# Six token chunks instead of three multiplied from the raw input in float32, at the start of a diffusion step

## The chip, the cores and the metric

The kernel runs on one core of a Trainium2 chip. The number that counts is the device time of one execution in microseconds; the kernel before takes 2201.28 us, the median of three runs from 2199.71 to 2201.73. A tenth of one per cent is therefore 2.2 us.

The engines are named as in the profile: PE (TensorE: matrix products; PEld its weight loads), DVE (VectorE), ACT (ScalarE), POOL (GpSimd) and SP, which issues nearly all of the transfers.

## The reference

One layer of a backbone works on 128 context tokens and 1024 latent tokens, 1152 in all, with 1024 channels. The layer starts like this, and this start is all that the change touches:

```python
sh1, sc1, gt1, sh2, sc2, gt2 = adaln(cond, p['w_mod'], p['b_mod'])   # silu(c) @ w_mod + b_mod
h = rmsnorm(x, p['g_norm_mix']) * (1.0 + sc1) + sh1
z = h @ p['w_in']        # columns: zq, zkv, zkpe, zmq, zmk, zmv, zgate, zmo, zbr
...
mv = zmv.reshape(B, S, MLSTM_HEADS, MLSTM_DV)     # 4 heads of 256 values
```

The context tokens have one modulation vector, the latent tokens another. After this come latent attention, a two-way chunked mLSTM that uses the values `mv`, a merge, a gated feed-forward block and a last norm.

Everything is float32, and the outputs are compared in float32. One value product for a chunk of 128 tokens and two heads is 128 x 1024 times 1024 x 512.

## The kernel before

**Two ways to multiply.** A product in float32 proper is one matmul instruction per 128 rows of the contraction. The other way splits each operand into a high part `h`, rounded to a shorter float32 (`hi`, line 69, on ACT), and the rest `l` (`lo`, line 75, on DVE), and adds three matmuls `h*h + h*l + l*h` (`mm3`, lines 98 to 100). The profile tells the two apart by their lines: L470 is the float32 product of the start, L98, L99 and L100 are the three of `mm3`.

**The nine chunks of the values.** `start` (line 329) makes the values of all nine 128-token chunks for two halves of the columns, `hp` 0 and 1: eighteen jobs, each of eight contraction steps `k`. They come in four groups, named in line 381 and put in order in line 382; each group runs over four pieces of weights, of 128 x 1024 and two steps `k` each:

- `GR`, half 0, chunks 1, 2, 3, from the raw input. For a latent token, `h` is `r * (x * A) + sh` with one factor `r` per token. So the product can be taken on raw `x` with the weights scaled by `A` (`ws`, line 510, ACT) before `r` is known, and `r` and the shift come in when the result leaves PSUM (`vout`, line 495, DVE). This group uses float32 proper (`rawmm`, L470).
- `GA`, half 1, chunks 5, 6, 7, split.
- `GB`, half 1, chunks 0, 1, 2, 3, 8, 4, split.
- `GC`, half 0, chunks 0, 5, 6, 7, 8, 4, split.

Chunk 4 lies across the middle of the tokens and is copied together by POOL (`copy4`, line 447, tile `c4`).

**What runs while.** The input arrives in four blocks `b` of two steps `k`, together with the modulation weights. For each block PE computes the modulation (`gemv`, lines 367 and 372), and ACT and DVE square the input for the norm (lines 403 and 405). After the last block, `stats` finds `r` (lines 411 to 420), and `modk` turns `x` into `h` in place: a multiplication on DVE (L435), an addition on ACT (L437), then `hi` and `lo`. The half of the tokens from 576 on (`j` = 1) is done first, since `GA` needs it; the other half is done while `GA` and `GB` run.

Results leave PSUM over three buffers `vs` (line 494) and SP's queue. PSUM has six banks for these products (`mm` in line 77). The weights of a piece have four split buffers, `wh` and `wl` of two pieces (`loadv`, line 392).

During `GB`, POOL also begins the four large differences of `t_ops` (line 568), which the next stage, `z_lat`, needs. The pieces of the next stage (`pair`, matmuls 128x288) follow directly on PE after `GC`.

**What sets the order.** The program is written in one stream; a scheduler with its own estimate of times then puts each engine's instructions into a fixed order. An engine works through its list strictly in that order, except for what the hardware overlaps. So a change of three lines can move instructions well away from those lines.

Of the kernel before, what the change touches and what calls it, by code (L numbers as in the profile page):

```python
# [19 lines left out]
P = 128  # L20
D = 1024
KD = 8
# [25 lines left out]
GT = T // 2  # L48
# [8 lines left out]
class K:  # L57
# [271 lines left out]
    def start(self, vp):  # L329


        nc, a, pp = self.nc, self.a, self.pp
# [14 lines left out]
        xv = lambda k, j: X[k // 4][j][:, k % 4]  # L347
# [30 lines left out]
                                        self.vec[:, self.V_GMIX + k:self.V_GMIX + k + 1], op0=ALU.add, op1=ALU.mult)  # L378
            nc.vector.tensor_copy(shs[:, 2 * b:2 * b + 2, 0:1], self.mod1[:, 2 * b:2 * b + 2, 1:2])
        nc.scalar.activation(sil[:, :, 0:2], self.silc, AF.Silu)  # L380
        GR, GA, GB, GC = (1, 2, 3), (5, 6, 7), (0, 1, 2, 3, 8, 4), (0, 5, 6, 7, 8, 4)
        order = [(0, GR, kk) for kk in range(4)] + [(hp, g, kk) for hp, g in ((1, GA), (1, GB), (0, GC)) for kk in range(4)]
        raw, wv = {}, {}

        def vload(i):
            if i < len(order):
                hp, _, kk = order[i]
                raw[i] = self.wp.tile([P, 4 * DV], F32, name=self.nm("wr"), tag="wr", bufs=self.wb[0])
                nc.sync.dma_start(raw[i], a["w_v"][hp][:, kk * 4 * DV:(kk + 1) * 4 * DV])

        def loadv(i):
            if i < len(order):
                w = [self.wp.tile([P, 4 * DV], R32, name=self.nm(n), tag="wo", bufs=self.wb[1]) for n in ("wh", "wl")]
                r = raw.pop(i)
                self.last = self.hi(w[0], r), self.lo(w[1], r, w[0])
                wv[i] = [t.rearrange("p (k f) -> p k f", k=2) for t in w]
# [34 lines left out]
        def modk(k, j):  # L431
            x = xv(k, j)
            for c, s in ((slice(0, TP), 0), (slice(TP, GT), 1)) if j == 0 else ((slice(0, GT), 1),):
                A, sh = self.A1[:, k, s:s + 1], self.mod1[:, k, s:s + 1]
                line("s", lambda: nc.vector.scalar_tensor_tensor(x[:, c], x[:, c], A, rbc[:, j * GT + c.start:j * GT + c.stop],  # L435
                                                                 op0=ALU.mult, op1=ALU.mult).ins, "l")
                line("a", lambda: nc.scalar.activation(x[:, c], x[:, c], AF.Identity, bias=sh).ins, "h")  # L437
            nm = f"B{k // 4 + 1}{j + 1}"
            if nm not in self.hop:
                self.hop[nm] = tuple(self.slot({"B11": 0, "B21": 8, "B22": 10}[nm] + e, [P, 4, GT], nm) for e in range(2))  # L440
            h, l = self.hop[nm]
            line("h", lambda: self.hi(h[:, k % 4], x))
            line("l", lambda: self.lo(l[:, k % 4], x, h[:, k % 4]))

        def copy4(k, j):
            for e in range(2):
                nc.gpsimd.tensor_copy(c4[:, e, k, 64 * j:64 * j + 64],
                                      self.hop[f"B{k // 4 + 1}{j + 1}"][e][:, k % 4, 0 if j else GT - 64:64 if j else GT])
# [7 lines left out]
        ps = {}  # L456

        def vmm(w, c, k):
            if k == 0:
                ps[c] = self.bank(pp, "mm")  # L460
            self.mm3(ps[c], hc(k, c), (w[0][:, k % 2], w[1][:, k % 2]), k == 0, k == KD - 1)

        def rawmm(b, sw, e):

            w = sw.rearrange("p (k f) -> p k f", k=2)
            k = 2 * b + e
            for c in GR:
                if k == 0:
                    ps[c] = self.bank(pp, "mm")
                nc.tensor.matmul(ps[c], xv(k, 0)[:, c * P:(c + 1) * P], w[:, e], start=k == 0, stop=k == KD - 1)  # L470

        shv = sp.tile([P, 512], F32, name="shv")

# [18 lines left out]
        def vout(hp, c, r=None, sh=None):  # L492
            vs = vp.tile([P, 2 * DV], F32, name=self.nm("vs"), tag="vs", bufs=3)
            if r is not None:
                nc.vector.scalar_tensor_tensor(vs, ps[c], r[:, c:c + 1], sh, op0=ALU.mult, op1=ALU.add)
            elif c % 2:
                nc.vector.tensor_copy(vs, ps[c])
            else:
                nc.scalar.copy(vs, ps[c])
            nc.sync.dma_start(self.d_v[c, :, 2 * hp:2 * hp + 2, :], vs.rearrange("p (h v) -> p h v", h=2))  # L500
# [4 lines left out]
        for b in range(4):  # L505
            gemv(b)
            sw = f32v(self.wp.tile([P, 4 * DV], R32, name=self.nm("ws"), tag="wo", bufs=self.wb[1]))
            for e in range(2):
                k = 2 * b + e
                nc.scalar.activation(sw[:, 512 * e:512 * e + 512], raw[b][:, 512 * e:512 * e + 512], AF.Copy, scale=self.A1[:, k, 1:2])  # L510
            square(b)
            rawmm(b, sw, 0)
            if b == 3:
                st = stats()
                r = next(st)
            rawmm(b, sw, 1)
            shift(b)
            raw.pop(b)
            vload(b + 4)
# [11 lines left out]
        for i in range(4, 12):  # L531
            if i > 4:
                vload(i + 3)
            loadv(i + 1)
            for k in (2 * (i % 4), 2 * (i % 4) + 1):
                if i < 8:
                    modk(k, 0)
                    copy4(k, 0)
                    copy4(k, 1)
                for c in order[i][1]:  # L540
                    vmm(wv[i], c, k)
            if i % 4 == 3:
                for c in order[i][1]:
                    vout(1, c)
        es.close()
        xp = es.enter_context(self.pool("x"))
        self.push(self.t_ops(X, xp))
        for i in range(12, len(order)):
            hp, g, kk = order[i]
# [1546 lines left out]
```

## Time and profile before

| | us |
|---|---|
| median of three runs | 2201.28 |
| the profiled execution | 2201.13 |
| its span, first to last instruction | 2199.4 |
| up to the first raw product | 16.7 |
| raw products of four blocks (`GR`) | 41.5 |
| bridge to the first split product | 7.9 |
| `GA` (72 split matmuls) | 18.7 |
| `GB` (144) | 38.0 |
| `GC` (144) | 32.6 |
| all that follows | 2044.0 |

In the rows of the profile, the first number is the start in us from the start of the span, the second the duration; `xN` is how many instructions a row merges, and the bracket at the end tells how long the engine had been idle before, and what ended that. A float32 matmul shows up as two records. The share of PE's clock that was granted is `PEclk`, 1.00 at full speed.

### The profile page before, as it was taken

The numbers are of one execution on the slowest core, as the hardware profiler recorded it, in microseconds if no ns is written. First come the engines' busy times: TensorE is split into PE (matmuls) and PEld (weight loads), VectorE is DVE, ScalarE is ACT, GpSimd is POOL, SyncE is SP. The second block draws the span as 40 slices with busy tenths as digits, with TensorE's granted clock in tenths as the row PEclk, the third lists the DMA queues.
The fourth block names the chain that finished last, engine by engine and source line by source line (L and its number), as shares of the span: only waits on it lengthen the run. The fifth ranks groups of instructions, "written<-read, shape, count | busy, mean of one in ns | idle before, by whom it ended". The sixth has DMA issues, their size and how long they took to land.

```text
span 2199.4 us, 36807 instructions
## 1 busy us (share of the span) xinstructions
PE 2057.0 (94%) x13495; PEld 1873.4 (85%) x13495; DVE 1528.7 (70%) x2700; ACT 935.4 (43%) x1850; POOL 996.6 (45%) x766
## 2 busy tenths in 40 slices
PE   7899989999989888999999999889999999989897
PEld 3689989989978775667776899879999999989897
DVE  3846656988744977566664648899645555799895
ACT  3533334555455534333433335544322222456464
POOL 0622124667435414444446535576776733421501
PEclk9999999999989997999999999899999999999898
DMA  8332335555489685222224664223556512557664
GB/s 314 103 120 83 104 99 162 164 175 187 143 284 326 198 271 153 70 78 71 84 72 116 209 206 145 76 95 123 189 171 196 176 61 85 173 168 253 220 203 129
DMA packets 233795, 343.89 MB, mean 156 GB/s; under 512 B 20079, under 2 KB 166735, under 8 KB 232463
## 3 DMA queue, kind: packets, MB, share of 16 engines
q1 hardware_dynamic: 225070, 331.88, 47.3%
q0 software_dynamic: 4848, 6.06, 1.1%
q10 hardware_dynamic: 3696, 3.61, 0.5%
q8 instruction: 106, 1.74, 0.3%
q14 instruction: 75, 0.61, 0.1%
HBM read 253.69 MB, written 87.80 MB: 155 GB/s over the span
## 4 chain that ended last, share of the span: by engine, by line
PE 47%; DVE 11%; DMA 8%; POOL 6%; issue 5%; ACT 1%; SPq 1%; DVEq 0%; POOLq 0%; ACTq 0%
PE mm L98 11%; PE mm L100 11%; PE mm L99 11%; DVE wo L75 4%; PE pv L1476 3%; DMA pr<-w_fo 3%; PE st L98 2%; PE st L99 1%; PE st L100 1%; PE mx L1398 1%; DVE sm L1400 1%; PE p L1102 1%; PE p L1107 1%; PE p L1104 1%; POOL ps L1773 1%
## 5 line engine op out<-in xcount | busy, mean ns | idle before, releaser
L100 PE MATMUL mm<-th,wo 128*128 128x288 f32 x1840 | 547.3, 298 | 15.1 <-DVE wo L75 14.8
L98 PE MATMUL mm<-th,wo 128*128 128x288 f32 x1840 | 548.7, 298 | 3.0 <-DVE zo L1702 1.1
L99 PE MATMUL mm<-tl,wo 128*128 128x288 f32 x1840 | 547.0, 297 | 0.0
L100 PEld LDWEIGHTS mm<-th,wo 128*128 128x128 f32 x1840 | 349.6, 190 | 19.2 <-DVE wo L75 18.6
L75 DVE TENSOR_TENSOR wo<-wr,wo 128x512 fp32r<-128x512 f32 (+1 forms) x317 | 315.0, 1009 | 54.5 <-ACT wo L69 51.7
L98 PEld LDWEIGHTS mm<-th,wo 128*128 128x128 f32 x1840 | 348.6, 189 | 4.9 <-issue 1.6
L99 PEld LDWEIGHTS mm<-tl,wo 128*128 128x128 f32 x1840 | 349.2, 190 | 0.1
L69 ACT ACTIVATE wo<-wr 128x512 fp32r<-128x512 f32 (+1 forms) x317 | 187.5, 608 | 141.6 <-PE mm L100 62.5
L75 DVE TENSOR_TENSOR wo<-ws,wo 128x512 fp32r<-128x512 f32 x188 | 187.9, 1002 | 64.8 <-ACT wo L69 64.7
L69 ACT ACTIVATE wo<-ws 128x512 fp32r<-128x512 f32 x188 | 116.5, 626 | 270.8 <-PE mm L100 158.1
L1445 POOL TENSOR_TENSOR es<-es,p 128x512 f32<-128x512 f32 x112 | 157.1, 1402 | 91.0 <-ACT p L1438 87.2
L100 PE MATMUL mm<-xh,wo 128*128 128x288 f32 x616 | 184.5, 301 | 9.0 <-DVE wo L75 8.9
L99 PE MATMUL mm<-xl,wo 128*128 128x288 f32 x616 | 184.6, 300 | 0.0
L98 PE MATMUL mm<-xh,wo 128*128 128x288 f32 x616 | 183.9, 299 | 0.2 <-ACT wo L69 0.2
L1686 POOL TENSOR_TENSOR ws<-wr,ws 128x512 f32<-128x512 f32 x47 | 61.8, 1316 | 226.6 <-DVE wo L75 221.2
L1438 ACT ACTIVATE p<-st 128x512 f32<-128x512 f32 (+1 forms) x152 | 87.6, 578 | 158.0 <-PE st L100 146.4
L1400 DVE TENSOR_REDUCE sm<-mx 128x1 f32<-128x384 f32 (+1 forms) x200 | 99.1, 539 | 66.0 <-PE mx L1398 65.1
L98 PE MATMUL mm<-B,wo 128*128 128x288 f32 x456 | 134.8, 296 | 2.2 <-DVE zo L1702 1.3
L100 PE MATMUL mm<-B,wo 128*128 128x288 f32 x456 | 134.8, 296 | 0.0
L99 PE MATMUL mm<-B,wo 128*128 128x288 f32 x456 | 134.8, 296 | 0.0
L722 POOL TENSOR_TENSOR wm<-wm,sr 128x512 f32<-128x512 f32 x64 | 100.8, 1578 | 65.4 <-DVE mj L721 63.4
L100 PEld LDWEIGHTS mm<-xh,wo 128*128 128x128 f32 x616 | 118.0, 192 | 11.5 <-DVE wo L75 11.2
(436 smaller groups left out, 5067.5 us busy)
## 6 DMA issues: line engine op xcount, KB each, us to landing
wr<-w_ff SPq DMA_DIRECT2D x56, 512.0 KB
wm<-wm SPq DMA_DIRECT2D x32, 512.0 KB
wr<-d_w SPq DMA_DIRECT2D x32, 512.0 KB
d_z<-zo SPq DMA_DIRECT2D x48, 288.0 KB
d_g<-uu SPq DMA_DIRECT2D x44, 288.0 KB
wr<-w_big SPq DMA_DIRECT2D x24, 512.0 KB
wr<-w_fo SPq DMA_DIRECT2D x24, 512.0 KB
pr<-w_fo SPq DMA_DIRECT2D x40, 256.0 KB
```

Source lines behind the costliest of these rows:

```text
L69: i = self.nc.scalar.activation(out, in_, AF.Copy)
L75: return self.nc.vector.tensor_sub(out, in_, f32v(hi)).ins
L98: mm(out, lhs[0], rhs[0], start=first, stop=False)
L99: mm(out, lhs[0], rhs[1], start=False, stop=False)
L100: self.pe = mm(out, lhs[1], rhs[0], start=False, stop=last).ins
L722: nc.gpsimd.tensor_tensor(w[:, n], w[:, n], sr[:, 1], op=ALU.mult)
L1102: self.pe = mm(p1, A[:, h], V[:, h], start=True, stop=not carried).ins
L1400: self.iv = nc.vector.tensor_reduce(sm[:, t, j:j + 1], s[:, :kc], axis=AX.X, op=ALU.max, negate=True).ins
L1438: self.ia = nc.scalar.activation(p[:, :n], st[:, :n], AF.Exp).ins
L1445: nc.gpsimd.tensor_tensor(U["sum"], U["sum"], p, op=ALU.add)
L1476: self.pe = nc.tensor.matmul(pv[g * AV:(g + 1) * AV, q0:q0 + w], v[:, kb[c]], U["P"][c][:, q0:q0 + w], start=c < 2, stop=c == U["nc"] - 1, ...
L1686: G.tensor_tensor(s4, a12, s2, op=ALU.subtract)
```

## The change

```diff
-        GR, GA, GB, GC = (1, 2, 3), (5, 6, 7), (0, 1, 2, 3, 8, 4), (0, 5, 6, 7, 8, 4)
-        order = [(0, GR, kk) for kk in range(4)] + [(hp, g, kk) for hp, g in ((1, GA), (1, GB), (0, GC)) for kk in range(4)]
+        GR, GA, GB, GC = (1, 2, 3, 5, 6, 7), (5, 6, 7), (0, 8, 4), (0, 1, 2, 3, 8, 4)
+        order = [(0, GR, kk) for kk in range(4)] + [(hp, g, kk) for hp, g in ((1, GA), (0, GB), (1, GC)) for kk in range(4)]
...
             for c in GR:
                 if k == 0:
                     ps[c] = self.bank(pp, "mm")
-                nc.tensor.matmul(ps[c], xv(k, 0)[:, c * P:(c + 1) * P], w[:, e], start=k == 0, stop=k == KD - 1)
+                j = int(c > 4)
+                nc.tensor.matmul(ps[c], xv(k, j)[:, c * P - j * GT:(c + 1) * P - j * GT], w[:, e], start=k == 0, stop=k == KD - 1)
...
             if i % 4 == 3:
                 for c in order[i][1]:
-                    vout(1, c)
+                    vout(order[i][0], c)
```

Chunks 5, 6, 7 of half 0 move from the split `GC` to the raw `GR`, which now fills all six banks. `GB` keeps three chunks of half 0; the six-chunk group is the last one, of half 1. Eighteen jobs stay eighteen; six are raw instead of three.

**PE, the second block of the start.** `mm_209` to `mm_219` are the accumulators of `GR`, `ws` its scaled weights, `mx` with `wm` the modulation product of the next block. Before:

```order
L470 MATMUL mm_209<-ws_245,x_17_141 128x512
L470 MATMUL mm_211<-ws_245,x_17_141 128x512
L470 MATMUL mm_213<-ws_245,x_17_141 128x512
L367 MATMUL mx_268<-wm_165,sil 32x512 x4
L372 MATMUL mx_279<-vec,rows_277 128x2 x4
```

and now:

```order
L471 MATMUL mm_209<-ws_254,x_17_141 128x512
L471 MATMUL mm_211<-ws_254,x_17_141 128x512
L471 MATMUL mm_213<-ws_254,x_17_141 128x512
L471 MATMUL mm_215<-ws_254,x_18_142 128x512
L471 MATMUL mm_217<-ws_254,x_18_142 128x512
L471 MATMUL mm_219<-ws_254,x_18_142 128x512
L372 MATMUL mx_294<-vec,rows_292 128x2 x4
```

Six raw matmuls per step `k` stand where three stood, and the second part of the modulation product, which stood between the raw products and L372, has moved ahead of the raw products.

**DVE, after the last raw product.** `vs` is a result on its way out, `x` times `A` and `rbc` the multiplication of `modk`, `b12l` the first low part that `GA` uses. Before:

```order
L495 SCALAR_TENSOR_TENSOR vs_435<-mm_213,y_358,shv 128x512
L418 TENSOR_SCALAR dg_408<-ident,y_358 128x128
L435 SCALAR_TENSOR_TENSOR x_18_142<-x_18_142,A_70,rbc 128x576 x2
L75 TENSOR_TENSOR b12l<-x_18_142,b12h 128x576
L435 SCALAR_TENSOR_TENSOR x_18_142<-x_18_142,A_70,rbc 128x576
```

and now:

```order
L496 SCALAR_TENSOR_TENSOR vs_462<-mm_213,y_382,shv 128x512
L418 TENSOR_SCALAR dg_435<-ident,y_382 128x128
L496 SCALAR_TENSOR_TENSOR vs_465<-mm_215,y_382,shv 128x512
L435 SCALAR_TENSOR_TENSOR x_18_142<-x_18_142,A_70,rbc 128x576 x2
L496 SCALAR_TENSOR_TENSOR vs_468<-mm_217,y_382,shv 128x512
L496 SCALAR_TENSOR_TENSOR vs_471<-mm_219,y_382,shv 128x512
L75 TENSOR_TENSOR b12l<-x_18_142,b12h 128x576
```

The fourth result goes out ahead of the first `modk`, the fifth and sixth ahead of the first low part.

**DVE, at the end of `GA`.** `vs_642` before and `vs_678` now are the first result of `GA`, the `wl` the low parts of weight pieces, `B` those of the modulated input, all for `GB`. Before:

```order
L497 COPY vs_642<-mm_477 128x512
L75 TENSOR_TENSOR B_82_470<-x_17_141,B_81_469 128x576
L435 SCALAR_TENSOR_TENSOR x_19_143<-x_19_143,A_70,rbc 128x128
L435 SCALAR_TENSOR_TENSOR x_19_143<-x_19_143,A_70,rbc 128x448
L497 COPY vs_648<-mm_485 128x512
L75 TENSOR_TENSOR wl_654<-wr_552,wh_653 128x1024
```

and now:

```order
L498 COPY vs_678<-mm_513 128x512
L75 TENSOR_TENSOR B_88_506<-x_17_141,B_87_505 128x576
L435 SCALAR_TENSOR_TENSOR x_17_141<-x_17_141,A_70,rbc 128x128
L435 SCALAR_TENSOR_TENSOR x_17_141<-x_17_141,A_70,rbc 128x448
L498 COPY vs_684<-mm_521 128x512
L75 TENSOR_TENSOR wl_690<-wr_588,wh_689 128x1024
L75 TENSOR_TENSOR B_88_506<-x_17_141,B_87_505 128x576
```

When `GA`'s first result goes out, DVE has one step `k` more of the modulated input still to make than before: the low part in the row behind it is that of `k` = 1, where it was that of `k` = 2.

Far behind, between 640 and 840 us of the profile, where the mLSTM and the attention's projections share PE, some 300 of the 12,800 matmuls stand in another order too, though no line of that stage is changed. But for one further pair of rows, nothing else on PE moves.

## The prediction

> **What bounds the kernel now.** I read the busy time by stage first, since the change sits in the first 160 us.
>
> ```profile
> 16.70:58.20 41.50, 38.27 (x153) 16.73 (x151) 17.39 (x51) 15.77 (x24) 0.00 (x0) 0.96 0.76 297
> 58.20:66.10 7.90, 3.55 (x21) 2.44 (x20) 5.03 (x7) 4.10 (x8) 0.00 (x0) 0.86 0.49 166
> 66.10:84.80 18.70, 18.65 (x73) 15.23 (x74) 18.02 (x27) 16.52 (x26) 12.60 (x20) 0.88 0.17 57
> 84.80:122.80 38.00, 34.36 (x146) 27.90 (x144) 25.64 (x23) 13.57 (x23) 29.38 (x17) 0.96 0.32 103
> 122.80:155.40 32.60, 32.60 (x145) 27.02 (x144) 14.74 (x11) 14.78 (x13) 3.83 (x3) 1.00 0.31 100
> ```
>
> After the length come the busy times of PE, PEld, DVE, ACT, POOL, then PE's clock. These stages are GR, the bridge, GA, GB, GC. In GR, PE is busy 38.3 of 41.5 us: only 3.2 us are free to take more raw products. GC is pure PE work. In GA, DVE is nearly as full as PE. Next, what PE waits for, in order of time:
>
> ```profile
> 16.73 6.79 PE L470 MATMUL mm<-ws,x 128*128 128x512 f32 x12
> 29.48 5.42 PE L470 MATMUL mm<-ws,x 128*128 128x512 f32 x12
> 41.56 1.26 ACT L403 ACTIVATE sqs<-x 128x576 f32<-128x576 f32 x2 [0.24 <-DMA x<-xT]
> 36.65 1.05 PE L372 MATMUL mx<-vec,rows 128*128 128x2 f32 x8 [0.76 <-ACT rows L369]
> 47.22 1.05 PE L372 MATMUL mx<-vec,rows 128*128 128x2 f32 x8 [0.76 <-ACT rows L369]
> 52.07 6.19 PE L470 MATMUL mm<-ws,x 128*128 128x512 f32 x12
> 66.15 0.79 PE L98 MATMUL mm<-wh,b12h 128*128 128x512 f32 x1 [3.32 <-ACT b12h L69]
> 105.14 0.79 PE L99 MATMUL mm<-wl,B 128*128 128x512 f32 x1 [3.64 <-DVE wl L75]
> ```
>
> The last input has landed by 41.6 us, yet the last raw products start at 52.1: the loads do not pace this phase, PE's own list does. The one wait inside GB, 3.64 us, is for a low part from DVE. Behind GC, PE goes straight on, and most of the remaining stages are dense on PE, so I pass a shift at 155.4 us to the end.
>
> **The raw products.** What one costs:
>
> ```profile
> 54.23 0.19 PEld L470 LDWEIGHTS mm<-ws,x 128*128 128x128 f32 x1 [0.24 <-issue]
> 56.38 0.19 PEld L470 LDWEIGHTS mm<-ws,x 128*128 128x128 f32 x1 [0.24 <-issue]
> 122.80 0.39 PE L98 MATMUL mm<-wh,B 128*128 128x512 f32 x1
> 155.44 0.29 PE L98 MATMUL mm<-B,wo 128*128 128x288 f32 x1
> ```
>
> Five records lie between the first two rows: 2.15 / 5 = 0.43 us each, and a float32 product has two (12 records for 6 products above): 0.853 us with 0.4267 a record. GC's 144 matmuls take 155.44 - 122.80 = 32.64 us: 0.2267 each, 0.68 for a split product. Three chunks of eight steps move, 24 products: **24 x 0.853 = 20.5 us** go into GR, 24 x 0.68 = **16.3 us** come off the split groups. So even in full exchange PE has 4.2 us more to do.
>
> What of the 20.5 is hidden? The two waits of 0.76 for ACT's `rows` copy go: the modulation product now stands ahead of the raw products, which cover the copy. Minus 1.5. The rest of the 3.2 us free (waits on A, the scaled weights) has the same order as before. **GR ends 19.0 us later**; bounds 17.3 (all free time filled) and 20.5.
>
> **The bridge.** Six results go out instead of three, over three buffers.
>
> ```profile
> 59.97 2.07 DVE L495 SCALAR_TENSOR_TENSOR vs<-mm,y,shv 128x512 f32<-128x512 f32 x3 [0.39 <-ACT shv L490]
> 63.17 1.55 DVE L435 SCALAR_TENSOR_TENSOR x<-x,A,rbc 128x576 f32<-128x576 f32 x2 [0.94 <-ACT rbc L420]
> 66.13 0.76 DVE L75 TENSOR_TENSOR b12l<-x,b12h 128x576 fp32r<-128x576 f32 x1 [1.41 <-ACT b12h L69]
> 152.24 0.59 ACT L499 COPY vs<-mm 128x512 f32<-128x512 f32 x1 [0.43 <-PE mm L100]
> 155.14 0.69 DVE L497 COPY vs<-mm 128x512 f32<-128x512 f32 x1 [1.53 <-DMA d_v<-vs]
> ```
>
> The last two rows price a buffer: filled at 152.83, free at 155.14, 2.3 us. Measured on the times of before, the first buffer is full at 60.7 and free at 63.0, the fourth result takes 0.7, and the first modulation starts at 63.75 instead of 63.17: **+0.6**, and the first split matmul with it. The fifth and sixth (1.4 us) fit the hole of 1.41 ahead of the first low part; without that cover they would cost up to 1.4 more.
>
> **GB.** Its 72 matmuls would take 16.3 us instead of 32.6, and 3.64 of wait could go as well. But what GB needs is made while it runs, and there POOL stands in DVE's way:
>
> ```profile
> 87.47 0.68 DVE L497 COPY vs<-mm 128x512 f32<-128x512 f32 x1
> 88.07 5.58 DVE L75 TENSOR_TENSOR wl<-wr,wh 128x1024 fp32r<-128x1024 f32 x1
> 94.28 0.94 DVE L435 SCALAR_TENSOR_TENSOR x<-x,A,rbc 128x128 f32<-128x128 f32 x2
> 95.14 0.75 DVE L75 TENSOR_TENSOR B<-x,B 128x576 fp32r<-128x576 f32 x1
> 95.81 0.94 DVE L435 SCALAR_TENSOR_TENSOR x<-x,A,rbc 128x128 f32<-128x128 f32 x2
> 96.67 5.71 DVE L75 TENSOR_TENSOR B<-x,B 128x576 fp32r<-128x576 f32 x1
> 105.72 1.25 DVE L75 TENSOR_TENSOR wl<-wr,wh 128x1024 fp32r<-128x1024 f32 x1
> 115.70 2.77 DVE L75 TENSOR_TENSOR wl<-wr,wh 128x1024 fp32r<-128x1024 f32 x1 [8.74 <-ACT wh L69]
> ```
>
> ```profile
> 87.02 5.55 POOL L568 TENSOR_TENSOR t<-x,x 128x2304 f32<-128x2304 f32 x1
> 96.21 5.55 POOL L568 TENSOR_TENSOR x<-x,x 128x2304 f32<-128x2304 f32 x1
> 107.03 5.13 POOL L568 TENSOR_TENSOR x<-x,t 128x2304 f32<-128x2304 f32 x1
> 112.24 5.16 POOL L568 TENSOR_TENSOR t<-x,x 128x2304 f32<-128x2304 f32 x1
> ```
>
> Three times a DVE subtraction that meets one of POOL's large differences ends 1.1 us or less after it: 93.65 behind 92.57, 102.38 behind 101.76, 118.47 behind 117.40. So each difference stops DVE for some 5.1 us. Before, GB had 38 us to swallow two of them.
>
> The Trainium skill (SBUF — State Buffer, "Who interferes with whom") states the rule: a DVE instruction with two SBUF inputs and a GpSimd one share a port pair, whoever starts first holds it to its end, and issue order decides. The three overlaps agree; if DVE always came first, the sum would go towards the first rival.
>
> Now DVE's new order, still on the times of before. GA ends at 84.8 + 0.6 = 85.35, and its first result goes out to 85.85. Steps, from start to start in the rows: a pair of modulations 0.86, a low part 0.7; a copy 0.6; a weight's low part 1.15 (1.25 in its row, less the 0.1 by which rows overlap). To 89.85: low part, pair, copy, weight, low part. By then the first half of `x` is complete (ACT adds after the pair), and POOL's first difference holds DVE to 95.05. Pair, weight, low part, pair: 98.6. The second difference: 103.75. Four low parts, two pairs, a weight: 109.4, the last operand of GB. POOL copies chunk 4's piece and starts the third difference at about 110. PE still has GB's last ten matmuls, and only then are the buffers of the weights two pieces back free for GC's first piece: ACT makes the high part by 112.4, DVE's low part waits for POOL until 115.2 and ends at 116.4. Ahead of that PE has done five high products, so 139 x 0.2267 = 31.5 remain, and 1.3 for PE's clock:
>
> ```profile
> 64.00:66.00 2.00, 0.00 (x0) 0.00 (x0) 0.72 (x1) 1.98 (x3) 0.00 (x0) 0.50 0.39 148
> 66.00:68.00 2.00, 1.85 (x4) 1.49 (x5) 1.87 (x3) 1.02 (x3) 1.84 (x3) 0.50 0.00 0
> 107.44 0.63 PE L98 MATMUL mm<-wh,B 128*128 128x512 f32 x1
> 107.86 0.59 PE L99 MATMUL mm<-wl,B 128*128 128x512 f32 x1
> ```
>
> After a pause the clock is at 0.50, matmuls come 0.42 apart, and after the pause at 101 this lasted from 105.14 to 108.3, some 6.5 matmuls at 0.2 too much. GC then ends at 116.4 + 31.5 + 1.3 = 149.2, where it ended at 155.4: **-6.2**, with the 0.6 in it. Bounds: without any wait 85.35 + 216 x 0.2267 = 134.3, that is -21.1; with the fourth difference also ahead of the weight, +5.2, that is -1.0.
>
> **The mLSTM stage**, whose order moved, I take at nothing: what is swapped are independent products of the same size.
>
> ```profile
> 600.00:640.00 40.00, 30.07 (x201) 29.63 (x200) 17.18 (x31) 15.40 (x38) 12.86 (x19) 0.83 0.75 245
> 640.00:840.00 200.00, 182.09 (x981) 155.25 (x981) 139.75 (x415) 103.86 (x304) 68.68 (x60) 0.95 0.85 268
> ```
>
> PE idles 17.9 us in 640 to 840. A reorder can take at most that; as a loss I bound it by a few of PE's waits there, 4 us.
>
> **Sum**: +19.0 - 6.2 = **+12.8 us**. The profiled execution took 2201.13 us (1.7 around its span), 0.15 below the median: 2201.3 + 12.8 = **2214 us**.
>
> **The rivals.**
> - *The exchange goes through.* POOL's differences fall where DVE has nothing that PE waits for, GB and GC run densely: 19.0 - 21.1 = -2.1, 2199 us, no change. For it: DVE copies from PSUM pass beside POOL (87.47 within 87.02 to 92.57), and the weights of GB's third piece come earlier in DVE's order than before. Against: three overlaps of three stopped a subtraction, and even without POOL, DVE's steps above take 13.8 us of the 16.3 that GB would last, so any meeting shows. One difference out of the way gives +7.7.
> - *The port goes to POOL twice in a row* before GC's first low part: +18.0, 2219 us. For it: the fourth difference followed the third by 0.08 us. Against: DVE waits already when the third ends.
> - *The other side: the reordered mLSTM stage gains.* If PE's 17.9 idle us there closed up, 2214 - 17.9 = 2196 us, faster; it decides from 17.2 us on. For it: 300 rows moved there. Against: its transfers run at 268 GB/s, and a new order brings no data earlier.
> - *A wait behind absorbs the delay.* PE idles 9.9 us in 600 to 640; if its end were set by something that does not hang on PE's front, 2214 - 9.9 = 2204, no change. Against: one list after the other is fed by PE's results.
>
> That raw work hides behind the loads I rule out (41.56 against 52.07); and the order of PE shows that the change does what it says.
>
> **How the numbers follow.** Forecast 0.63, POOL twice 0.17, the exchange 0.10, the absorbed delay 0.05, the mLSTM gain 0.05. About 0.2%, 4.4 us, is what a measurement here tells from no change. Slower: 0.80 with both slower cases. Same: 0.15. Faster: 0.05. The forecast's own range is +7 to +17, with one difference more or less and GR's bounds; for 8 in 10 I add the POOL case above and some of the exchange below: 2202 to 2221.
>
> **What would show it.** Right: 96 records of raw products (L471 in the new numbering), the last raw products ending near 77 us; the first split matmul near 86; two DVE subtractions of over 5 us inside GB and a wait of PE for a low part at GC's start; the first 128x288 matmul near 168. Wrong: GR shorter than 58 us (raw products cheaper or hidden), GB near 16 us (POOL not in the way), or a difference that arises behind 168 us.

## The result and the profile after

The changed kernel takes 2220.24 us, the median of four runs from 2214.56 to 2221.53, beside 2201.51 us for the kernel before: a ratio of 1.0080, 95% interval 1.0061 to 1.0099. A second set of six runs gave 2216.95 us beside 2202.23, a ratio of 1.0067 (1.0051 to 1.0083). So the change makes the kernel 15 to 19 us slower. The first profiled execution took 2219.8 us, with a span of 2218.0.

The windows of the changed kernel, cut at its own stages (raw group, bridge, `GA`, `GB`, `GC`; the columns are those of the prediction's first fence):

```profile
15.70:75.40 59.70, 57.99 (x201) 26.55 (x199) 17.21 (x51) 15.82 (x25) 0.00 (x0) 0.95 0.55 213
75.40:85.50 10.10, 3.54 (x21) 2.43 (x20) 7.01 (x10) 4.11 (x8) 0.00 (x0) 0.88 0.45 156
85.50:104.00 18.50, 18.46 (x72) 15.11 (x73) 16.77 (x24) 15.23 (x23) 11.78 (x19) 0.88 0.27 87
104.00:135.40 31.40, 23.40 (x80) 16.90 (x79) 27.65 (x25) 16.33 (x27) 23.36 (x18) 0.84 0.32 108
135.40:166.50 31.10, 31.10 (x138) 25.72 (x138) 18.28 (x10) 12.76 (x10) 10.48 (x4) 1.00 0.28 94
```

The raw group now fills 59.7 us, where it filled 41.5. The fourth stretch takes 31.4 us with PE busy for only 23.4: that is where half of the 16.3 us taken off the split groups is given back. (It ends where PE goes on at 135.4; `GC`'s first matmul stands at 131.76, so `GB` itself takes 27.7 us.) PE's rows in order of time:

```profile
15.72 11.82 PE L471 MATMUL mm<-ws,x 128*128 128x512 f32 x24
63.90 1.05 PE L479 MATMUL mx<-wr,shs 128*32 128x512 f32 x4
64.88 10.57 PE L471 MATMUL mm<-ws,x 128*128 128x512 f32 x24
85.54 0.79 PE L98 MATMUL mm<-wh,b12h 128*128 128x512 f32 x1 [5.52 <-ACT b12h L69]
113.82 0.79 PE L100 MATMUL mm<-wh,B 128*128 128x512 f32 x1 [3.06 <-DVE B L75]
122.93 0.50 PE L100 MATMUL mm<-wh,B 128*128 128x512 f32 x1 [2.88 <-DVE B L75]
134.89 0.49 PE L99 MATMUL mm<-wl,B 128*128 128x512 f32 x1 [1.68 <-DVE wl L75]
166.54 0.29 PE L98 MATMUL mm<-B,wo 128*128 128x288 f32 x1
```

Four blocks of 24 records are the 48 raw products; the last ends at 64.88 + 10.57 = 75.45. In the fourth stretch PE waits three times for over 1 us for a low part from DVE, twice in `GB` and once at the start of `GC`, and what holds DVE stands in DVE's and POOL's rows:

```profile
77.16 2.07 DVE L496 SCALAR_TENSOR_TENSOR vs<-mm,y,shv 128x512 f32<-128x512 f32 x3 [0.39 <-ACT shv L491]
81.90 0.75 DVE L496 SCALAR_TENSOR_TENSOR vs<-mm,y,shv 128x512 f32<-128x512 f32 x1 [2.48 <-DMA d_v<-vs]
108.09 5.67 DVE L75 TENSOR_TENSOR B<-x,B 128x576 fp32r<-128x576 f32 x1
117.25 5.63 DVE L75 TENSOR_TENSOR B<-x,B 128x576 fp32r<-128x576 f32 x1
131.74 9.19 DVE L75 TENSOR_TENSOR wl<-wr,wh 128x1024 fp32r<-128x1024 f32 x2 [3.42 <-ACT wh L69]
```

```profile
107.60 5.55 POOL L569 TENSOR_TENSOR t<-x,x 128x2304 f32<-128x2304 f32 x1 [0.64 <-DMA d_v<-vs]
116.79 5.47 POOL L569 TENSOR_TENSOR x<-x,x 128x2304 f32<-128x2304 f32 x1
128.58 5.17 POOL L569 TENSOR_TENSOR x<-x,t 128x2304 f32<-128x2304 f32 x1
133.83 6.02 POOL L569 TENSOR_TENSOR t<-x,x 128x2304 f32<-128x2304 f32 x1
```

The two subtractions of 5.67 and 5.63 us end at 113.76 and 122.88, each 0.6 us behind one of POOL's differences, and PE goes on 0.05 us later, as predicted.

The first 128x288 matmul starts 11.1 us later than before. The kernel ends 18.6 us later. So in this execution 7.5 us arise behind the part that was changed, and they are the main question of the experiments. To place them, the same instruction of PE was looked up in each trace and in the first trace of before; the table gives the difference of its start in us (the middle one of all the instructions in the stretch, which is on the times of before). It holds all the profiles, those of the experiments too; `changed, again` and `before, again` are second executions of the two kernels.

| kernel | at 70 (`GA`) | 156 to 170 | 1000 to 1150 | 1480 to 1540 | 1750 to 1850 | 2100 to 2190 |
|---|---|---|---|---|---|---|
| changed | 19.3 | 11.1 | 9.0 | 12.2 | 18.2 | 18.8 |
| changed, again | 24.7 | 16.8 | 12.2 | 11.8 | 17.0 | 14.7 |
| before, again | 0.4 | 0.5 | 0.6 | 0.6 | 0.6 | 0.6 |
| raw_extra | 17.9 | 19.8 | 18.9 | 19.1 | 23.2 | 24.5 |
| order_3_6_3 | 20.8 | 7.2 | 7.7 | 10.6 | 15.4 | 14.4 |
| late_diff | 19.5 | 6.8 | 2.9 | 5.4 | 11.7 | 11.9 |
| late_diff_before | -0.8 | -0.9 | -4.3 | -3.6 | -4.0 | -4.5 |
| before_prep_once | 1.0 | 0.6 | -1.5 | -1.3 | -3.7 | -5.7 |
| after_prep_once | 19.9 | 11.7 | 9.7 | 13.3 | 10.5 | 9.4 |
| after_pad12 | 19.1 | 10.9 | 5.5 | 5.7 | 7.2 | 5.3 |
| before_pad24 | 1.3 | 1.4 | 1.3 | 1.9 | 4.6 | 7.5 |
| before_pad40 | 0.0 | 0.1 | -3.4 | -1.7 | 3.3 | 6.6 |
| before_pad52 | -0.1 | -0.1 | -3.6 | -3.0 | 3.2 | 4.2 |

### The profile page after: what moved, and what is told of

It is laid out like the page before. It is cut to its first block, busy times and chain, and to the rows that moved or that the text cites. A ratio compares the mean times of both kernels' runs of the same rounds, so it can differ in the third digit from the quotient of the medians.

```text
span 2218.0 us, 36751 instructions
## 1 busy us (share of the span) xinstructions
PE 2064.8 (93%) x13471; PEld 1870.4 (84%) x13471; DVE 1534.1 (69%) x2701; ACT 935.7 (42%) x1849; POOL 998.1 (45%) x766
## 3 DMA queue, kind: packets, MB, share of 16 engines
q8 instruction: 106, 1.74, 0.3%
## 4 chain that ended last, share of the span: by engine, by line
PE 48%; DVE 12%; DMA 8%; POOL 6%; issue 5%; ACT 2%; SPq 1%; DVEq 0%; POOLq 0%; ACTq 0%
PE mm L98 11%; PE mm L100 11%; PE mm L99 11%; DVE wo L75 5%; PE pv L1477 3%; DMA pr<-w_fo 3%; PE st L98 2%; PE st L99 2%; PE st L100 2%; PE mx L1399 1%; PE p L1103 1%; POOL wm L723 1%; DVE sm L1401 1%; DMA wm<-wm 1%; PE p L1105 1%
## 5 line engine op out<-in xcount | busy, mean ns | idle before, releaser
L100 PE MATMUL mm<-th,wo 128*128 128x288 f32 x1840 | 547.7, 298 | 14.2 <-DVE wo L75 13.9
L69 ACT ACTIVATE wo<-ws 128x512 fp32r<-128x512 f32 x188 | 116.4, 626 | 278.6 <-PE mm L100 146.9
```

The costliest lines, as they stand in the source:

```text
L69: i = self.nc.scalar.activation(out, in_, AF.Copy)
L100: self.pe = mm(out, lhs[1], rhs[0], start=False, stop=last).ins
```

## The experiments

### The raw products alone, and the order of the groups

The first kernel leaves before as it is and adds 24 raw products whose results nobody uses. The second is the changed kernel with the groups in the old order: three, six, three.

```diff
-            for c in GR:
+            for c in GR + (5, 6, 7):
```

```diff
-        GR, GA, GB, GC = (1, 2, 3, 5, 6, 7), (5, 6, 7), (0, 8, 4), (0, 1, 2, 3, 8, 4)
-        order = [(0, GR, kk) for kk in range(4)] + [(hp, g, kk) for hp, g in ((1, GA), (0, GB), (1, GC)) for kk in range(4)]
+        GR, GA, GB, GC = (1, 2, 3, 5, 6, 7), (5, 6, 7), (0, 1, 2, 3, 8, 4), (0, 8, 4)
+        order = [(0, GR, kk) for kk in range(4)] + [(hp, g, kk) for hp, g in ((1, GA), (1, GB), (0, GC)) for kk in range(4)]
```

> The kernel before, with 24 further raw float32 products (chunks 5, 6, 7, the eight steps) that are computed and thrown away; nothing else moves, so the split products of before all stay. Theory (the raw phase is PE's own list): the last raw product ends near 75.4 us instead of 58.2 (+17.2, as in the changed kernel), the bridge is not longer since no fourth result waits for a buffer, GB and GC take 38.0 and 32.6 as before, and the first 128x288 matmul starts near 172.6 instead of 155.4; total about 2219 us. Rival (raw products hide behind the loads of the input): the last raw product ends before 64 us and the total stays under 2206. On the 7 us that the changed kernel lost in the feed-forward stage: if the changed order in the mLSTM stage caused them, they are absent here, since that order is the one of before; if they hang on how the stage's transfers and PE happen to line up, a drift of up to 7 us can appear here too.

> The changed kernel with the two last groups exchanged: six raw chunks, then split groups of three, six and three chunks (GB again 0, 1, 2, 3, 8, 4 of half 1, GC 0, 8, 4 of half 0). The same 96 raw records and the same number of split products. Theory (the three-chunk GB is too short to cover DVE's and POOL's work): the first split matmul at 85.5 as in the changed kernel, GB takes 38 us again, GC 16.3 instead of 32.6, the first 128x288 matmul near 159 to 161 instead of 166.5; total 5 to 8 us under the changed kernel, unless the high and low parts of the next stage come late, since GC gives them 16 us less: then up to 6 us of it are lost. Rival (the cost is the raw products' surcharge and the bridge, whatever the order): within 2 us of the changed kernel at the first 128x288 matmul.

Measured: raw_extra 2223.76 us, ratio 1.0099 (1.0080 to 1.0118); order_3_6_3 2213.24 us, ratio 1.0052 (1.0032 to 1.0071). PE's rows of the first:

```profile
64.16 11.29 PE L471 MATMUL mm<-ws,x 128*128 128x512 f32 x24
83.34 0.80 PE L98 MATMUL mm<-wh,b12h 128*128 128x512 f32 x1 [3.32 <-ACT b12h L69]
175.22 0.29 PE L98 MATMUL mm<-B,wo 128*128 128x288 f32 x1
```

The raw group ends at 75.45, 17.2 us later than before: the extra products are not hidden; of their 20.5 us, 17.2 come through. The bridge takes 83.34 - 75.45 = 7.9 us, as before, since only three results go out over the three buffers. In the changed kernel it takes 10.1: the 2.2 us more come from six results, not from the raw products. From there to the first 128x288 matmul another 2.6 us came up (175.22, where 172.6 was expected): 0.7 in each of `GA` and `GB`, 1.1 in `GC`. One premise of the expectation did not hold: raw_extra's order in the mLSTM stage is not that of before either. Between 620 and 860 us PE has another matmul than before at 388 places of its list (415 in the changed kernel, counted the same way), so this run can't tell whether that order costs anything.

The order of the groups costs 166.54 - 162.05 = 4.5 us at the first 128x288 matmul (its row in order_3_6_3 starts at 162.05), although that kernel began its split groups 1.2 us later. With a group of six in front, two of POOL's differences fall into it unseen, and PE waits for a low part for over 1 us only once:

```profile
126.96 0.79 PE L99 MATMUL mm<-wl,B 128*128 128x512 f32 x1 [3.99 <-DVE wl L75]
162.05 0.29 PE L98 MATMUL mm<-B,wo 128*128 128x288 f32 x1
```

With three in front, three of the four show.

### The differences moved behind

Two kernels, on the changed one and on before, start POOL's four large differences late: at `GC`'s first step a small copy on POOL waits for the low part of its second piece of weights, and the differences stand behind that copy.

```diff
-        self.push(self.t_ops(X, xp))
+        gate = xp.tile([P, 1], F32, name="gate")
...
+                if k == 0:
+                    self.late = nc.gpsimd.tensor_copy(gate, f32v(wv[13][1][:, 0, 0:1])).ins
+                    self.push(self.t_ops(X, xp))
...
-        sub = lambda o, x, y: G.tensor_tensor(o, x, y, op=ALU.subtract)
+        def sub(o, x, y):
+            with self.tc.issue_after(self.late):
+                G.tensor_tensor(o, x, y, op=ALU.subtract)
```

> The changed kernel with POOL's four large differences queued behind a one-column POOL copy that needs the low part of GC's second weights piece, so that they run in GC instead of GB. Theory (each difference holds DVE's subtractions for 5.1 us): no DVE subtraction of over 3 us before GC; GB ends near 121 instead of 132, the first 128x288 matmul near 155 instead of 166.5; total 9 to 12 us under the changed kernel, less up to 5 if the differences then come late for the next stage. Rival (DVE's own list bounds GB, POOL does not matter): the first 128x288 matmul within 2 us of 166.5.

> The kernel before with the same delay of POOL's differences. Theory: the one wait inside GB (3.64 us, and 1.3 for PE's clock behind it) goes, the first 128x288 matmul near 150.5 instead of 155.4, total about 2196; with differences late for the next stage up to 5 us worse. Rival (the differences do not bound GB): first 128x288 matmul within 1 us of 155.4.

Measured: late_diff 2212.89 us, ratio 1.0052 (1.0035 to 1.0070); late_diff_before 2202.73 us, ratio 1.0002 (0.9990 to 1.0013). PE's rows of late_diff:

```profile
85.63 0.80 PE L98 MATMUL mm<-wh,b12h 128*128 128x512 f32 x1 [5.51 <-ACT b12h L69]
159.46 0.58 PE L98 MATMUL mm<-B,wo 128*128 128x288 f32 x1 [5.81 <-DVE vs L498]
```

and DVE's row that it waits behind, with POOL's:

```profile
150.66 7.45 DVE L75 TENSOR_TENSOR tl<-x,th 128x2304 fp32r<-128x2304 f32 x1
158.64 0.68 DVE L498 COPY vs<-mm 128x512 f32<-128x512 f32 x1
```

```profile
150.26 5.44 POOL L574 TENSOR_TENSOR t<-x,x 128x2304 f32<-128x2304 f32 x1
```

From the first split matmul to the end of the split groups there lie 288 matmuls, 288 x 0.2267 = 65.3 us. Here they are done by 159.46 - 5.81 = 153.65, 68.0 us: 2.7 us lost. In the changed kernel they take 81.0: 15.7 us lost, 8.0 of them in PE's waits behind 85.54; the clock makes most of the rest, since it stood at 0.50 behind the two waits in `GB`, from 113.8 to 120.6 and from 124.1 to 127.5 us. So the differences are what keeps `GB` and `GC` from the exchange that the diff would give. They don't vanish, though: moved behind, they hold DVE's own large subtraction and the copy behind it, PE waits 5.81 us, and of 13 us gained 4.3 are left at 156 to 170 us. The time is 7 us below the first set of the changed kernel and 4 below the second, where 9 to 12, or up to 5 less, were expected. In before, where about 5 us were expected, nothing is left: the first 128x288 matmul comes 6.3 us sooner (149.18), 5.4 of it is given back at once, and the time is the same.

### Both kernels again

> The unchanged kernel once more, for a second profile and more times. In the first profile of the changed kernel the delay is 12.2 us at 1530 us (times of before) and 18.2 us at 1755 us: 6 us more arise while the feed-forward weights are prepared (POOL's differences of w_fo, one round after another, each load, differences and store in a row). The theory that this is jitter of the loads: this profile shows a lag against the first one that differs between 1530 and 1755 us by some us, of either sign. The rival, that the preparation runs at one speed for a given kernel: the lag changes by less than 1 us between 1530 and 1755 us. Both: ratio 1.000.

> The changed kernel once more. Ratio 1.0085 by the earlier runs. Jitter theory: the delay against the first profile of before is 12 us at 1530 us again, and between 1530 and 1755 us anything from -2 to +6 us is added. The rival (the change lengthens the preparation): +5 to +6.5 again. In the start, both: last raw products end near 75.4, first split matmul near 85.5, first 128x288 matmul near 166.5.

Measured: before_again 2201.88 us, ratio 1.0001 (0.9989 to 1.0014); after_again 2216.95 us, as above. In the table, before again stays at 0.6 from 1000 us to the end, and the changed kernel again gains 5.2 us between 1480 and 1850. But its lag at the end, 14.7, is below the 16.8 that it had at 156 to 170: all that arises behind the changed part adds up to +7.5 us in one execution and to -2.1 in the other. The step between 1480 and 1850 is what both have. All five profiles with six raw chunks and the loads in place show such a step, 4.1 to 6.3 us; before again and late_diff_before show none. Jitter of single executions doesn't sort itself by kernel like that.

The start differs between the two executions of the changed kernel by 5 us, most of it by the clock:

```profile
65.80 1.92 PE L479 MATMUL mx<-wr,shs 128*32 128x512 f32 x4
67.65 12.79 PE L471 MATMUL mm<-ws,x 128*128 128x512 f32 x24
```

The same records took 1.05 and 10.57 us in the first one. The granted clock over the two stretches (the column behind the five busy times), in the second execution and in the first:

```profile
65.80:72.00 6.20, 6.20 (x10) 2.04 (x10) 5.33 (x22) 1.66 (x3) 0.00 (x0) 0.50 0.46 154
63.90:70.00 6.10, 6.10 (x17) 2.53 (x17) 5.24 (x22) 1.86 (x3) 0.00 (x0) 1.00 0.53 175
```

Of the 5 us between the two, 3 are left at 1000 us and none at 1480: the second execution loses lag between 640 and 1000, the first gains some between 1150 and 1480.

### The preparation of the feed-forward weights without its loads

Between 1530 and 1755 us `prep` makes 24 rounds: load a piece of `w_fo`, four differences on POOL, store. One round is issued behind the other, and POOL also makes differences that PE's matmuls need. Two kernels load only in the first round and leave out the other 23 loads, so what they prepare are not the real weights.

```diff
                 n = min(256, HK * P - c0)
-                r = sp.tile([P, 2, 2, 256], F32, name=self.nm("pr"), tag="pr")
-                with self.tc.issue_after(self.ld):
+                if p == 0 and c0 == 0:
+                    r = sp.tile([P, 2, 2, 256], F32, name=self.nm("pr"), tag="pr")
+                    with self.tc.issue_after(self.ld):
...
```

> Before, but the preparation of the feed-forward weights loads its piece of w_fo only in the first of its 24 rounds and makes all the differences from that piece (so the later layer's output uses wrong weights; everything else is computed as before). Its rounds then have no load to wait for. Expected of both theories: the 57.5 us in which POOL waits for these loads go; PE's own waits in 1630 to 1750 us were only 2 us, so the time falls by 0 to 3 us: 2199 to 2203.

> The changed kernel with the same cut: loads of w_fo in the first round of the preparation alone (the later layer's weights are wrong, all else is computed). If the 6 us that are added between 1530 and 1755 us come out of the preparation's loads, the delay against the same cut of before is the 12 us that it has at 1530 us: 11 to 13 us at the end. The rival, that they come from elsewhere in the feed-forward stage: 18 to 19 us as without the cut.

Measured: before_prep_once 2200.60 us, ratio 0.9991 (0.9976 to 1.0005); after_prep_once 2210.97 us, ratio 1.0038 (1.0025 to 1.0051). 10.4 us lie between the two, close to the 11 to 13 expected if the loads are the cause. In the table the step is gone: 13.3 at 1480, 10.5 at 1750, and against the same kernel made from before 14.6 and 14.2. So the step comes out of these loads, though from 1480 us on every engine has the same instructions in the same order in the changed kernel as in before.

### The place of the instruction fetches

What does differ there are PE's instruction fetches. The instruction queue of the changed kernel's page, and the first line of busy time of before, the changed kernel and after_pad12, in this order:

```profile
q8 instruction: 106, 1.74, 0.3%
```

```profile
PE 2057.0 (94%) x13495; PEld 1873.4 (85%) x13495; DVE 1528.7 (70%) x2700; ACT 935.4 (43%) x1850; POOL 996.6 (45%) x766
```

```profile
PE 2064.8 (93%) x13471; PEld 1870.4 (84%) x13471; DVE 1534.1 (69%) x2701; ACT 935.7 (42%) x1849; POOL 998.1 (45%) x766
```

```profile
PE 2057.1 (93%) x13495; PEld 1863.1 (85%) x13495; DVE 1531.8 (69%) x2701; ACT 933.9 (42%) x1849; POOL 998.6 (45%) x766
```

106 packets of 1.74 MB are 16.4 KB each. PE has 2 x 13,471 = 26,942 matmuls and weight loads; spread over the 106 packets that is 254 to a packet, and 65 bytes each. The Trainium skill (Perfetto Trace Analysis, "The 4-stage abstract model") has 64 bytes to an instruction; the trace agrees. The changed kernel's list is 48 instructions shorter than that of before, all of it in the first 170 us, and so every later packet is fetched at another place of the work. Four kernels move that place and nothing else (with 52 products one small copy on DVE stands a place further forward): throwaway products on constants at PE's very start, where PE waits 7.6 us anyway.

```diff
             g = self.bank(pp, "mx")
+            for _ in range(12 if b == 0 else 0):
+                nc.tensor.matmul(g[0:32, 0:2], self.ones[:, 0:32], self.ones[:, 0:2], start=True, stop=True)
             for k in range(KD):
```

> The changed kernel with 12 throwaway float32 products of 32x2 on constants at PE's very start, where PE waits 7.7 us for its first operand; the bank is overwritten by the first real product, and no other instruction on any engine moves. The five profiles with six raw chunks add 4 to 6 us between 1530 and 1755 us, the three with three raw chunks none, though the instructions there stand in one order in all of them; with the preparation's loads cut out, none. What does differ there is where PE's own instruction stream is fetched (packets of the instruction queue, one in some 16 us): in the changed kernel 2 to 4 us later in the work than before, since its list up to there is 48 instructions shorter (24 more products of 4, 72 fewer of 2). The 12 products add 48 and put the fetches back in place. Theory that the place of the fetches decides how late the preparation's loads land: nothing is added between 1530 and 1755 us, lag at the end 12 to 13 us, ratio 1.005 to 1.006. Rival, that it is anything else: 4 to 6 us are added as before, ratio 1.007 to 1.008.

> Before with 24 such throwaway products in the same place, 96 instructions, which is what the kernel with 24 extra raw products has more (that one added 4 us between 1530 and 1755 us). Nothing else moves; the products lie in the 7.6 us in which PE waits, so the start does not change. Theory of the fetches: their places move as in that kernel, 4 us are added between 1530 and 1755 us, ratio 1.002. Rival: nothing is added, ratio 1.000.

> Before with 52 throwaway products at PE's start: 208 instructions. 24 products (96 instructions) moved the fetches by 6 us towards the front, so 208 move them by 13; the fetches lie 16 to 17 us apart, so they come to lie 3 to 4 us later than in before, which is where the changed kernel has them. Theory of the fetches: the pattern of the preparation's rounds is that of the changed kernel (the seventh round 9.6 us, the thirteenth 9.7, the fifteenth 12.6, in before 8.4, 8.5 and 11.3), 5 us are added between 1530 and 1755 us, and the time rises to 2206 to 2209, ratio 1.002 to 1.004. Rival, that only some paddings matter by chance or the added work does: 0 or 3 us as with 24, another pattern.

> Before with 40 such products, 160 instructions: the fetches come 10 us earlier, or 6 us later, than in before, a place that none of the kernels had. This is tried for a better place than that of before. Theory of the fetches: some other time between 2196 and 2209; a gain of over 0.1% would be a version better than both. Rival: 2201, as before.

Measured: after_pad12 2208.73 us, ratio 1.0036 (1.0023 to 1.0048); before_pad24 2208.12 us, 1.0025 (1.0014 to 1.0035); before_pad52 2208.13 us, 1.0022 (1.0010 to 1.0034); before_pad40 2207.31 us, 1.0029 (1.0015 to 1.0044). Twelve products that compute nothing make the changed kernel faster, outside both of its intervals; 24, 40 or 52 make before slower by 5 to 6 us, by the ratios. In before_pad52 the 104 records end before PE's first operand is there:

```profile
1.14 5.71 PE L366 MATMUL mx<-ones 128*32 128x2 f32 x104 [1.14 <-POOL ones L173]
7.33 3.64 PE L369 MATMUL mx<-wm,sil 128*32 128x512 f32 x16 [0.49 <-ACT sil L382]
```

The fetches, read from the trace in steps of 1 us, on the times of before (each kernel's lag at 1480 to 1540 taken off, so that the later ones are right to 2 us), with the step of the table:

| kernel | fetches for PE between 1545 and 1655 us | step, 1480 to 1850 |
|---|---|---|
| before | 1548 1563 1580 1596 1613 1632 1647 | |
| after_pad12 | 1549 1562 1579 1596 1613 1631 1647 | 1.5 |
| late_diff_before | 1549 1562 1580 1596 1614 1632 1647 | -0.4 |
| changed | 1551 1566 1583 1600 1617 1634 1652 | 6.0 |
| before_pad52 | 1551 1567 1583 1599 1617 1634 1652 | 6.2 |
| order_3_6_3 | 1551 1566 1582 1599 1617 1633 1651 | 4.8 |
| late_diff | 1551 1567 1583 1599 1617 1634 1652 | 6.3 |
| raw_extra | 1557 1575 1590 1607 1623 1640 | 4.1 |
| before_pad24 | 1560 1574 1592 1608 1624 1640 | 2.7 |
| before_pad40 | 1552 1568 1586 1603 1619 1638 | 5.0 |

The new order of the mLSTM stage doesn't sort the kernels like that: before_pad52 has the order of before there and a step of 6.2, after_pad12 has the new one and a step of 1.5. The rounds of before_pad52 are those that were expected, too: from load to load 9.5 us in round 7, 9.7 in round 13 and 12.8 in round 15 (counted from 0), where before takes 8.4, 8.6 and 11.4.

That round 15 shows how it goes. SP's rows of before and of the changed kernel (`pr` the load, `d_w` the store that ends a round):

```profile
1667.61 1.49 SPq L1767 DMA_DIRECT2D pr<-w_fo  x2
1678.48 0.37 SPq L1777 DMA_DIRECT2D d_w<-ps  x1
```

```profile
1682.85 1.49 SPq L1768 DMA_DIRECT2D pr<-w_fo  x2
1695.22 0.37 SPq L1778 DMA_DIRECT2D d_w<-ps  x1
```

POOL's first difference of that round, in before, the changed kernel, before_pad52 and after_pad12:

```profile
1672.54 0.74 POOL L1772 TENSOR_TENSOR ps<-pr 128x256 f32<-128x256 f32 x1 [0.67 <-DMA pr<-w_fo]
```

```profile
1689.27 0.74 POOL L1773 TENSOR_TENSOR ps<-pr 128x256 f32<-128x256 f32 x1 [2.17 <-DMA pr<-w_fo]
```

```profile
1674.80 0.74 POOL L1774 TENSOR_TENSOR ps<-pr 128x256 f32<-128x256 f32 x1 [2.13 <-DMA pr<-w_fo]
```

```profile
1678.82 0.74 POOL L1775 TENSOR_TENSOR ps<-pr 128x256 f32<-128x256 f32 x1 [0.76 <-DMA pr<-w_fo]
```

and the DMA queues while that load is under way: the changed kernel from 1682.8 to 1689.3, before_pad52 from 1668.4 to 1674.9, and before from 1667.6 to 1672.6.

```profile
q1 hardware_dynamic: 1321, 1.79, 84.1%
q8 instruction: 1, 0.02, 1.5%
```

```profile
q1 hardware_dynamic: 1319, 1.79, 87.6%
q8 instruction: 1, 0.02, 0.9%
```

```profile
q1 hardware_dynamic: 1149, 1.36, 89.2%
```

In the changed kernel and in before_pad52 a fetch falls into this load's flight, and the load is there 6.4 us after its issue; in before and after_pad12 none does, and it is there after 4.9 and 5.0 us (1672.54 - 1667.61; SP's row of after_pad12 starts at 1673.78).

One round could be chance, but the twelve profiles that load in all 24 rounds hold 288 such loads. From the issue to POOL's first difference the 48 loads into which a fetch for PE falls took 5.7 us in the median, the other 240 took 4.5. Before, before again, late_diff_before and after_pad12 have at most one such load each, and their 24 loads add up to 108.0 to 108.6 us; the eight others have two to nine, and 111.9 to 117.1 us.

Of such delays POOL's lateness is made, and PE waits for what POOL makes late. ACT, in before and in the changed kernel, waits for an operand that POOL makes behind its differences of round 14, and the wait of PE that grows most between the two kernels is for the copy that ACT makes next:

```profile
1666.45 0.63 ACT L69 ACTIVATE wo<-ws 128x512 fp32r<-128x512 f32 x1 [7.64 <-POOL ws L1686]
1667.42 0.40 PE L98 MATMUL mm<-th,wo 128*128 128x288 f32 x1 [0.81 <-ACT m L1714]
```

```profile
1681.70 0.63 ACT L69 ACTIVATE wo<-ws 128x512 fp32r<-128x512 f32 x1 [9.29 <-POOL ws L1687]
1682.67 0.40 PE L98 MATMUL mm<-th,wo 128*128 128x288 f32 x1 [1.93 <-ACT m L1715]
```

That the place of the fetches decides the step is shown by the kernels that move nothing else. That a fetch delays a load because both pass through the same DMA engines is what I take from it, and it is not shown. It would fit that the packet itself took 1.6 and 0.9 us in the two windows above (1.5% and 0.9% of 16 engines over 6.5 us). But the longer windows also moved 0.4 MB more of other transfers at the same rate, and whether these are cause or consequence the windows don't tell.

The expectation for after_pad12 was met in the step (1.5 us; the expectation was none, its rival 4 to 6) and missed in the sum: 5.3 us instead of 12 to 13 at the end of the profile, 7.7 in the medians. Of that, 3 us are gained between 640 and 1000 us, in the mLSTM stage. There late_diff, late_diff_before, before_pad40, before_pad52 and the changed kernel again gain about 3 as well, order_3_6_3 loses 3, the others stay within 1; this goes with no place of the fetches, and what sets it is open. Another 3 us are not lost between 1150 and 1480 us: there the changed kernel, order_3_6_3, late_diff and after_prep_once gain 2.5 to 3.6 us of lag, after_pad12 and the changed kernel again none. That is open too. Open is also why the kernels with 24 and 40 products lose another 3 us behind 1850.

No version was faster than before.

## Why the prediction was right, and where it was wrong

It forecast 2214 us, slower, with a range of 2202 to 2221. The medians of 2220 and 2217 lie inside it, in its upper half. That 2220 does is partly luck: the range reached up there for a case that did not happen, POOL taking the port twice in a row. Its steps:

- **24 raw products of 0.853 us go into the raw group: right.** raw_extra shows it alone. The group ends 17.2 us later in the first profile, 22.2 in the second (67.65 + 12.79 = 80.44), 19.0 by the forecast. The two waits of 0.76 us are gone, as foreseen. Most of the rest is PE's clock, which the forecast had taken from one execution: the last block of before (6.19 us, beside 5.42 for the same 12 records earlier) had lost 0.8 us by it, that of the first profile nothing, that of the second 2.2.
- **The bridge, +0.6 us: mis-sized.** It takes 10.1 instead of 7.9. The fourth result waits 2.48 us for a buffer: the first one is full at 77.85 (a third of the 2.07 us behind 77.16) and free at 81.90, 4.0 us later, where the two rows near `GC`'s end had given 2.3.
- **`GB` shortens by less than its work, since POOL's differences stop DVE: right.** It takes 27.7 us, where its matmuls alone would take 16.3. Two subtractions of over 5 us stand where they were expected, the wait at `GC`'s start came at 134.89 (forecast: 116.4 + 19.0 = 135.4), and the first 128x288 matmul at 166.54 (forecast: 168.2). Late_diff shows that the differences are the cause. As the rule in the Trainium skill (SBUF — State Buffer, "Who interferes with whom") has it, whoever starts first keeps the ports: 5.67 us for a subtraction that takes 0.7 alone.
- **The clock, 1.3 us behind that wait: not needed.** The wait was 1.68 us instead of 3.64, and the clock stood at 1.00 behind it. It fell behind the two waits in `GB` instead, where it cost nothing at the end, as PE had to wait for DVE again. With this, the smaller raw group (-1.8) and the longer bridge (+1.6), errors of either sign add up to only -1.7 us at 166.54: the front came out closer than its terms. In the second profile, 16.8 us late there, it was off by 4.
- **The mLSTM stage at nothing: right within what can be told.** The lag is 8.8 at 640 us and 9.0 at 1000. Kernels with the order of before move there between +0.3 and -3.6 us, those with the new order between +3.1 and -3.0.
- **"I pass a shift at 155.4 us to the end": wrong.** Up to 168 us the forecast was off by 1.7. Behind it the lag went from 11.1 to 18.8 us in the first profile and from 16.8 to 14.7 in the second; a difference that arises behind 168 us was what the prediction had named as a sign of being wrong. Both have 5 to 6 us in the preparation of the feed-forward weights. The step that failed took a stage whose instructions and their order stay the same to take the same time. What the runs showed in its place: a load there takes 5.7 instead of 4.5 us when a packet of PE's instructions falls into its time, and the place of these packets had moved by 48 instructions, 1400 us earlier. What moves the lag by 3 us elsewhere behind 168 us stays open.
- **The rivals.** The exchange did not go through. POOL did not get the port twice in a row: DVE's low part for `GC` came between its third and its fourth difference (PE goes on at 134.89, and the fourth took 6.02 us, where it had taken 5.16), so the case of 2219 us, though its number is near, is not what happened. Neither of the two gains came: the lag falls by 2 us between 170 and 600, not by 9.9, and the reordered stage gave nothing in the first profile and 2.5 us in the second, which kernels without the reorder gain as well.

## What to carry to other kernels

When work is moved between engines' idle times, ask what makes the operands: here PE could have done the same work in 15.7 us less, and what it lost went to waits for one engine that another engine's large operation had locked out, and to the low clock behind these waits. Price a stage that nobody touched with its spread as well, not at zero: where PE already waits at the end of a chain of loads (0.81 us in before), even the number of instructions issued long before decides some us. A change of a few us on such a kernel should be timed with a few harmless paddings of the instruction list beside it, so that luck in the fetches is not taken for the change.

## What the runs showed of the hardware

- PE's instructions come in during the run, as packets of 16.4 KB for 254 instructions, one every 14 to 19 us while PE works on 128x288 matmuls. A load of 512 KB with such a packet in its flight was there after 6.4 us, without it after 4.9; over twelve profiles the medians are 5.7 and 4.5.
- Added instructions that do nothing, issued in 5.7 us of PE's idle time, cost 5 us some 1500 us later (before_pad52), or gave some back (after_pad12).
- The granted clock behind the same stretch of small products differs between executions of one kernel: the last 24 raw records took 10.57 us in one and 12.79 in the other, and the four before them 1.05 and 1.92.
- Two executions of the changed kernel were 5 to 6 us apart in the first 170 us and level at 1480: a delay at the start need not reach the end in full, and one at the end need not come from there.
